# Dilated attention: class scores of exactly the blocks within reach, and class values with key tiles outside and classes inside

## The chip, the cores and the metric

The kernel runs on one NeuronCore of a Trainium2 chip. A core has TensorE for matrix products (PE in the profile, its weight loads PEld), VectorE (DVE), ScalarE (ACT), GpSimd (POOL), and the queue of SyncE (SP), which issues the DMAs of this kernel. The metric is the time of one execution in microseconds on the device; lower is better. The kernel before took 1236.35 us (median of 3 runs, 1234.39 to 1236.84).

## What is computed

One layer of a decoder for 1024 tokens of width 1024 in float32: a norm, one input projection, two mixers side by side (a gated delta rule with 4 heads of 128, and a dilated attention with 8 heads of 64), an output projection with a residual, a second norm, a gated MLP of width 2816 with a short convolution, and a last norm. The change touches the dilated attention alone. Each query at position t sees the keys of three branches, and the branches' sums are merged by their softmax denominators:

```
DIL_PATTERNS = ((128, 1), (512, 4), (2048, 16))      # (window, dilation)
...
for window, dil in DIL_PATTERNS:
    # keys t, t - dil, t - 2*dil, ... t - window, of the same head
    num, den, m = band_attention(stride(q), stride(k), stride(v), window // dil)
...
m_all = max(ms);  w_i = exp(m_i - m_all)
out = sum(w_i * num_i) / sum(w_i * den_i)
```

So a query sees all keys of the last 128 positions, and further back only keys whose distance is a multiple of 4: keys of its own class, where a token's class is its position modulo 4.

## The kernel before, in words

**Staging.** All activations lie with the channel on the partitions and the token along the free dimension. The stages follow one another on TensorE: the input projection ("dense"), the delta rule's chains, the attention, the output projection, the MLP up and down. They overlap: while the attention waits for its softmax, TensorE works on dense products that are left (the columns z of the projection, the a columns of later head pairs, and the first products of the output projection).

**The order on TensorE.** It is written out by a planner, the class Weave (line 46). Each stage is a generator that yields how long it would wait; the planner advances the ready stream with the lowest level (line 111) and books modelled costs: `product` (line 88) for TensorE, `account` (line 78) for the other engines (a fixed part and a part per element, lines 148 to 154; for ScalarE 0.12 us and 0.00085 us per element, for GpSimd 0.15 and 0.0021). A dense step is three matmuls of 512 columns (`mm3`, line 196) with a modelled 0.2135 us each. `mm` (line 188) stamps the order, so it is kept on TensorE. The slacks PSLACK and TSLACK (lines 38 and 39) let class and near values, and turns, come somewhat before the modelled time of their input. The attention has level 5, the dense products 9, the output projection 8 (lines 1491 to 1496).

**The attention** (from line 892) goes over 4 pairs of heads (pi), each with two halves of the sequence (hh = 0, 1), each half with four blocks of 128 queries (n = 4*hh + u, u = 0 to 3), taken two at a time. Inside a block the tokens are stored class by class, 32 tokens to a class. `advance` (line 1004) runs a pipeline: turn the pair before, score this pair, then the values of the pair before. The steps:

- `scores` (904): for each block, each head e of the pair against the near keys (the block and the one before it, up to 256 keys). The far keys are taken by class: 4 classes of 32 queries each against the same class of the earlier blocks, `far` columns, with weights of 64x32 at eight places of the array (line 924). `far` is 64*(n//2): 0, 0, 64, 64, 128, 128, 192, 192 for n = 0 to 7. A block with even n thereby also scores the class keys of block n - 1, which its near keys hold already; the mask puts these 32 columns to minus 1e30.
- `softmax` (929): VectorE adds the mask `mk` to the scores and finds the row's extreme in one instruction over `wd` = far + near columns, ScalarE takes the exponential with a sum, VectorE scales by the reciprocal. `mk` (line 1523) is 896 columns wide, one row of factors for even n and one for odd n.
- `turn` (946): transposes on TensorE in tiles of 128 columns into a bank; VectorE copies the near part to `pt`, ScalarE copies the far part, one instruction for all far tiles, 128 partitions, to `pb` (line 963). The tile `pb` holds for each head the far probabilities [key of class, u, key tile b, query], with one key tile for hh = 0 and two for hh = 1.
- `values` (966): the near values into the bank `po` (weights 128x64: one head's 64 channels).
- `merge_classes` (975): at the end of a group of four blocks, the class values are added to `po`: for each class c, for each part (key tile b, rows of it, first block u), for each head. For hh = 0 there is one part (64 rows, blocks 2 and 3); for hh = 1 two (tile 0: 128 rows, four blocks; tile 1: 64 rows, blocks 2 and 3).
- `give` (989): VectorE copies `po` out, SP writes it to the DRAM tensor `mixer`.

The tiles `pb` have four slots (tag "qa"), two tiles to a group, so a group's slots come free with the class values of the group before last.

Lines 139 and 141 are the planner's two calls to an engine, and 189 and 193 the two stamps of a product and a transpose; so the profile's rows are told apart by the tiles' names, not by lines. A bank of PSUM has the name `ps` in the attention's rows: `ps<-pb,vc` is a class value, `ps<-pt,vn` a near value, `ps<-kT,qT` a score, `ps<-ident,sm` a transpose, `ps<-xhi,whi`, `ps<-xlo,whi` and `ps<-xhi,wlo` the dense products.

Of the kernel before, what the change touches and what calls it, by code (L numbers as in the profile page):

```python
# [15 lines left out]
P = 128  # L16
# [5 lines left out]
NEG = -1.0e30  # L22
# [122 lines left out]
def hybrid_layer(tc, I, out):  # L145
# [22 lines left out]
    def A(name, tag, dt=F32, shape=(P, 1024)):  # L168
        if tag in TURNS:
            i = turns[tag] = turns.get(tag, -1) + 1  # L170
            tag = TURNS[tag][i % len(TURNS[tag])]
        return tile_(lp, shape, dt, name, tag, SLOTS[tag])
# [719 lines left out]
    def attention():  # L892
        for h in range(2):
            yield from wv.until(("c", h, NCH - 1))
        mk = A("mk", "go", shape=(P, 896))
        sy.dma_start(mk, I["mk"])
        for h in range(H):
            yield from wv.until(("o", h))
        for g in range(2):
            yield from wv.until(("V", g))  # L900
        yield from wv.until(("a", 0, 1))
        cur = att_load(0)

        def scores(pair):

            for it, tag in zip(pair, ("asc", "atr")):
                n = it["n"]
                it["k0"] = max(n - 1, 0) * P
                it["near"] = (n + 1) * P - it["k0"]
                it["far"] = 64 * (n // 2)  # L910
                it["wd"] = it["far"] + it["near"]
                it["ps"] = [bank(tag) for _ in range(2)]
            yield wv.need(*pair[0]["ps"], *pair[1]["ps"], pair[0]["q"], pair[0]["k"])
            for it in pair:
                n, k0, far, wd = it["n"], it["k0"], it["far"], it["wd"]
                for e, er in enumerate(HALVES):
                    mm(it["ps"][e][:, far:wd], it["q"][er, n * P:(n + 1) * P], it["k"][er, k0:k0 + wd - far],
                       0.00085 * (wd - far))
            for it in pair:
                n, far = it["n"], it["far"]  # L920
                for c in range(4 if far else 0):
                    o = slice(32 * c, 32 * c + 32)
                    for e, er in enumerate(HALVES):
                        mm(it["ps"][e][o, :far].rearrange("p (n u) -> p n u", u=32),
                           it["q"][er, n * P + 32 * c:n * P + 32 * c + 32], by_block(it["k"])[er, :far // 32, c, :],
                           0.00022 * far, tile_position=(64 * e, 32 * c))
                softmax(it)

        def softmax(it):
            pss, wd = it.pop("ps"), it["wd"]  # L930
            sm = it["sm"] = A("sm", "dv*", shape=(P, 2, 512))
            mx = tile_(sp, [P, 4], F32, "mx", "mx", 4)
            mn, den = mx[:, :2], mx[:, 2:]
            end = 896 if it["n"] % 2 else 448
            for e in range(2):
                uv.tensor_tensor_reduce(out=sm[:, e, :wd], in0=pss[e][:, :wd], in1=mk[:, end - wd:end], scale=-0.125,
                                        scalar=-NEG, op0=OP.add, op1=OP.min, accum_out=mn[:, e:e + 1])
            for e in range(2):
                ua.activation(sm[:, e, :wd], sm[:, e, :wd], AF.Exp, bias=mn[:, e:e + 1], scale=-1.0,
                              accum_out=den[:, e:e + 1])  # L940

            uv.reciprocal(den, den)
            for e in range(2):
                uv.tensor_scalar(sm[:, e, :wd], sm[:, e, :wd], den[:, e:e + 1], None, op0=OP.mult)

        def turn(pair):
            pts = A("pt", "dv*", shape=(P, 4, 256))
            for b, (it, tag) in enumerate(zip(pair, ("asc", "atr"))):
                sm, near, far = it["sm"], it["near"], it["far"]
                nf = -(-far // P)  # L950
                it["pt"] = []
                for e in range(2):
                    pt = pts[:, 2 * b + e, :]
                    it["pt"].append(pt)
                    pp = bank(tag)
                    yield wv.need(pp, sm, slack=TSLACK[b])
                    for i in range(near // P):
                        tp(pp[:, i * P:(i + 1) * P], sm[:, e, far + i * P:far + (i + 1) * P])
                    for i in range(nf):
                        tp(pp[:, near + i * P:near + (i + 1) * P], sm[:, e, i * P:(i + 1) * P])  # L960
                    uv.tensor_copy(pt[:, :near], pp[:, :near])
                    if nf:
                        ua.activation(it["pb"][e][:, it["u"], :nf, :].rearrange("p b t -> p (b t)"),
                                      pp[:, near:near + nf * P], AF.Copy)

        def values(pair):
            yield wv.need(pair[0]["po"], *pair[0]["pt"], slack=-PSLACK)
            for it in pair:
                u = it["u"]
                for i in range(it["near"] // P):  # L970
                    for e, er in enumerate(HALVES):
                        mm(it["po"][er, u * P:(u + 1) * P], v8(it["vn"])[:, it["k0"] // P + i, er],
                           it["pt"][e][:, i * P:(i + 1) * P], 0.11, u == 0 and i == 0, False, skip_group_check=True)

        def merge_classes(g):
            vcv = g["vc"].rearrange("p (b c d) -> p b c d", b=2, c=4)
            po, hh = g["po"], g["hh"]
            yield wv.need(*g["pb"], slack=-PSLACK)


            parts = (((0, 128, 0), (1, 64, 2)) if hh else ((0, 64, 2),))
            for c in range(4):
                for b, rows, u in parts:
                    for e, er in enumerate(HALVES):
                        mm(po[er].rearrange("p (u t) -> p u t", u=4)[:, u:, 32 * c:32 * c + 32],
                           vcv[:rows, b, c, er], g["pb"][e][:rows, u:, b, 32 * c:32 * c + 32], 0.11 - 0.028 * u,
                           False, c == 3 and b == hh, skip_group_check=True)

        def give(g):
            po, hh = g["po"], g["hh"]  # L990
            oT = tile_(sp, [P, 512], F32, "oT", "t2", 2)
            ve.tensor_copy(oT.rearrange("p (n u c) -> p n c u", n=4, c=4),
                           po.rearrange("p (n c u) -> p n c u", n=4, c=4))
            if g["pi"] < 3 or hh == 0:
                sy.dma_start(mixer[4 + g["pi"]][:, half(hh)], oT)
            else:
                last["oT"] = oT
            if hh == 1:
                wv.done.add(("o", 4 + g["pi"]))


        pipe = []

        def advance(pair):
            done = pipe.pop() if pipe else None
            if done is not None:
                yield from turn(done)
            if pair is not None:
                yield from scores(pair)
                pipe.append(pair)  # L1010
            if done is not None:
                yield from values(done)
                if done[1]["u"] == 3:
                    yield from merge_classes(done[0]["g"])
                    give(done[0]["g"])

        for pi in range(4):
            q, k, vn, vc = cur
            for hh in range(2):
                if hh == 1 and pi < 3:  # L1020
                    yield from wv.until(("a", pi + 1, 1))
                    cur = att_load(pi + 1)
                po = bank("ch")
                pb = [A("pb", "qa", shape=(P, 4, 1 + hh, P)) for _ in range(2)]
                if pi == 3 and hh == 1:
                    wv.done.add("last group")
                g = dict(po=po, pb=pb, hh=hh, pi=pi, vc=vc)
                for u in (0, 2):
                    yield from advance([dict(n=4 * hh + i, u=i, q=q, k=k, vn=vn, po=po, pb=pb, g=g)
                                        for i in (u, u + 1)])  # L1030
        yield from advance(None)
        wv.done.add("attention")
# [470 lines left out]
def host_inputs(inputs):  # L1503
# [5 lines left out]
    def tile_of(c):  # L1509
# [10 lines left out]
    near = levels[np.where(d < 0, 0, (d <= 128).astype(int) + (d % 4 == 0) + (d % 16 == 0))]  # L1520
    du = u32[:, None] - np.arange(32)[None, :]
    far = {e: levels[(128 * e + 4 * du <= 512).astype(int) + (du % 4 == 0)] for e in range(2, 8)}
    mk = np.concatenate([far[e] for e in range(6, 1, -1)] + [np.full((128, 32), NEG), near]
                        + [far[e] for e in range(7, 1, -1)] + [near], axis=1)
    j = np.arange(128)
    a = {
        "xT": f["x"][0].T,
# [32 lines left out]
```

## Time and profile before

| what | value |
|---|---|
| runs | 1234.39, 1236.35, 1236.84 us |
| the profiled execution's own time | 1232.33 us |
| its span, first to last instruction | 1230.2 us |
| mean granted TensorE clock | 0.995 |
| instructions | 17841, of them 6848 matmuls |
| TensorE, VectorE, ScalarE, GpSimd busy | 1206.7, 948.1, 570.7, 47.9 us |

How to read the profile: times are microseconds from the span's start, and each row of a group gives line, engine, operation, what is written from what, the shape (partitions x elements), how often, the busy time, the mean duration in ns, and after the second bar the engine's idle time just before and what ended it. In the timeline a row is start, duration, and the instructions merged into it. Matmuls are pipelined and their ends are modelled, so the difference of two starts is the better measure of what one takes. In a row of a stretch, after its limits and length, stand the busy time and number of instructions of each engine, the granted clock, and the share and rate of the DMAs.

### The profile page before, as it was taken

What the parts mean: (1) busy time and instruction counts of PE and PEld (TensorE: products, weight loads), DVE (VectorE), ACT (ScalarE), POOL (GpSimd) and SP (SyncE); (2) the same over time, 40 slices, a digit from 0 to 9 for tenths busy, and PEclk for the clock granted to TensorE, in tenths of its full rate; (3) what the DMA queues carried; (4) which work ended last, traced back from release to release, by engine and by line L of the source; (5) the groups of instructions that cost most, each with busy time, mean ns of one, the idle gap of its engine ahead of it and who ended that gap; (6) DMA issues with size and microseconds to landing.
All of it is one profiled execution on the core that took longest, in us unless ns stands there. A gap on an engine that the chain in (4) does not pass through costs nothing.

```text
span 1230.2 us, 17841 instructions
## 1 busy us (share of the span) xinstructions
PE 1206.7 (98%) x6848; PEld 992.2 (81%) x6848; DVE 948.1 (77%) x1522; ACT 570.7 (46%) x1099; POOL 47.9 (4%) x34
## 2 busy tenths in 40 slices
PE   9999999999999998999999999999999999999996
PEld 7878887888877776788888888888888888788886
DVE  7675964566377768577888889889898889899875
ACT  7393344356343345455544445444454553344441
POOL 0211010003100000000000000000000000000000
PEclk9999999999999999999999999999999999999998
DMA  6325251345722403343232231231322397545623
GB/s 231 104 90 154 83 154 71 122 136 167 238 74 95 121 27 111 129 153 117 74 103 88 66 103 61 94 101 53 103 76 79 108 373 254 172 153 183 195 86 137
DMA packets 85798, 155.02 MB, mean 126 GB/s; under 512 B 21168, under 2 KB 36176, under 8 KB 85712
## 3 DMA queue, kind: packets, MB, share of 16 engines
q1 hardware_dynamic: 85712, 153.87, 38.7%
q8 instruction: 54, 0.88, 0.3%
q14 instruction: 32, 0.26, 0.1%
HBM read 117.91 MB, written 35.93 MB: 125 GB/s over the span
## 4 chain that ended last, share of the span: by engine, by line
PE 83%; DVE 9%; DMA 4%; issue 2%; ACT 2%; POOL 0%; SPq 0%; POOLq 0%; DVEq 0%; ACTq 0%
PE ps L189 43%; PE pa L189 18%; PE pc L189 9%; PE dw L189 9%; PE ps L193 3%; DVE pr L139 2%; DMA wd<-in_wd 2%; DMA r<-upark 1%; DVE x1h L139 1%; DVE wd L139 1%; DVE kT L139 1%; DVE sm L141 1%; ACT dec L139 1%; PE warm L189 1%; DVE r L139 0%
## 5 line engine op out<-in xcount | busy, mean ns | idle before, releaser
L189 PE MATMUL dw<-pr 128*128 128x512 f32 (+1 forms) x984 | 213.2, 377 | 2.6 <-DVE x1h L139 1.9
L189 PEld LDWEIGHTS dw<-pr 128*128 128x128 f32 x984 | 176.1, 188 | 38.7 <-DVE x1h L139 3.6
L189 PE MATMUL ps<-xhi,whi 128*128 128x512 f32 x384 | 160.1, 417 | 0.0
L189 PE MATMUL ps<-xhi,wlo 128*128 128x512 f32 x384 | 150.5, 392 | 0.0
L189 PE MATMUL ps<-xlo,whi 128*128 128x512 f32 x384 | 150.1, 391 | 0.0
L189 PE MATMUL pa<-T,pair 128*128 128x512 f32 x528 | 127.0, 389 | 0.0
L189 PEld LDWEIGHTS pa<-T,pair 128*128 128x128 f32 x528 | 99.0, 188 | 20.5
L189 PEld LDWEIGHTS ps<-xhi,wlo 128*128 128x128 f32 x384 | 72.2, 188 | 16.1 <-DVE wlo L139 0.3
L189 PEld LDWEIGHTS ps<-xhi,whi 128*128 128x128 f32 x384 | 72.4, 189 | 14.9 <-issue 2.6
L189 PEld LDWEIGHTS ps<-xlo,whi 128*128 128x128 f32 x384 | 72.6, 189 | 11.2
L139 ACT ACTIVATE u<-pa 128x512 f32<-128x512 f32 x44 | 26.3, 598 | 110.7 <-PE pa L189 110.7
L139 DVE SCALAR_TENSOR_TENSOR y<-xu,fcw,y 128x1023 f32<-128x1023 f32 (+1 forms) x44 | 56.4, 1281 | 25.7 <-ACT y L139 25.6
L139 ACT ACTIVATE whi<-wst 128x1024 fp32r<-128x1024 f32 (+2 forms) x42 | 42.9, 1022 | 69.7 <-PE ps L189 64.1
L141 ACT ACTIVATE sm<-sm,mx 128x320 f32<-128x320 f32 (+4 forms) x64 | 36.1, 565 | 63.1 <-DVE mx L141 63.1
L189 PE MATMUL pc<-B,pair 128*128 128x512 f32 x264 | 63.4, 389 | 0.0
L189 PE MATMUL pa<-B,A 128*128 128x512 f32 x264 | 63.4, 389 | 0.0
L189 PE MATMUL pc<-T,S 128*128 128x512 f32 x264 | 63.4, 389 | 0.0
L189 PE MATMUL pa<-T,S 128*128 128x512 f32 x264 | 63.4, 389 | 0.0
L139 DVE TENSOR_TENSOR wst<-wst 128x512 f32<-128x512 f32 x88 | 60.4, 687 | 0.7
L189 PE MATMUL ps<-B,pair 128*128 128x512 f32 x252 | 60.5, 389 | 0.0
L139 DVE TENSOR_TENSOR wlo<-wst,whi 128x1024 fp32r<-128x1024 f32 (+2 forms) x42 | 49.4, 1175 | 12.1 <-ACT whi L139 12.0
L189 PEld LDWEIGHTS pa<-B,A 128*128 128x128 f32 x264 | 49.6, 188 | 10.3
(237 smaller groups left out, 2347.9 us busy)
## 6 DMA issues: line engine op xcount, KB each, us to landing
wst<-in_wu SPq DMA_DIRECT2D x44, 512.0 KB, 3.8
wd<-in_wd SPq DMA_DIRECT2D x44, 512.0 KB, 3.9
upark<-y SPq DMA_DIRECT2D x22, 512.0 KB, 3.8
wst<-in_wi SPq DMA_DIRECT2D x21, 512.0 KB, 3.7
r<-upark SPq DMA_DIRECT2D x11, 512.0 KB, 8.0
r<-upark SPq DMA_DIRECT2D x22, 256.0 KB, 7.0
wa<-in_wd SPq DMA_DIRECT2D x22, 256.0 KB, 2.8
wst<-in_wv SPq DMA_DIRECT2D x8, 512.0 KB, 3.6
```

The lines of the kernel that those rows point to most:

```text
L139: return getattr(eng, op)(*a, **kw)
L141: return getattr(eng, op)(*a, **kw)
L189: tc.stamp_issue_order_token(nc.tensor.matmul(dst, lhs, rhs, start=start, stop=stop, **kw).ins, TOKEN)
L193: tc.stamp_issue_order_token(nc.tensor.transpose(dst, src, ident).ins, TOKEN)
```

## The change

Four things, which belong together:

- `far` becomes 32*max(n - 1, 0): 0, 0, 32, 64, 96, 128, 160, 192 for n = 0 to 7, so class scores are made of exactly the blocks before the near ones.
- `mk` becomes 448 columns wide; the rows of even and odd n end alike, and the masked columns are gone.
- ScalarE's copy of the far part is made tile by tile, and only as many partitions as there are keys (32, 64, 96 or 128). The places of `pb` that no copy fills now, but that the class values read, are set to zero by GpSimd when the tile is taken: 32 partitions by 128 elements, once for each `pb` tile of an hh = 0 group and twice for each of an hh = 1 group.
- `merge_classes` loops over the parts outside and over the classes inside.

```diff
-        mk = A("mk", "go", shape=(P, 896))
+        mk = A("mk", "go", shape=(P, 448))
...
-                it["far"] = 64 * (n // 2)
+                it["far"] = max(n - 1, 0) * 32
...
-            end = 896 if it["n"] % 2 else 448
             for e in range(2):
-                uv.tensor_tensor_reduce(out=sm[:, e, :wd], in0=pss[e][:, :wd], in1=mk[:, end - wd:end], scale=-0.125,
+                uv.tensor_tensor_reduce(out=sm[:, e, :wd], in0=pss[e][:, :wd], in1=mk[:, 448 - wd:], scale=-0.125,
                                         scalar=-NEG, op0=OP.add, op1=OP.min, accum_out=mn[:, e:e + 1])
...
                     uv.tensor_copy(pt[:, :near], pp[:, :near])
-                    if nf:
-                        ua.activation(it["pb"][e][:, it["u"], :nf, :].rearrange("p b t -> p (b t)"),
-                                      pp[:, near:near + nf * P], AF.Copy)
+                    for i in range(nf):
+                        rows = min(far - i * P, P)
+                        ua.activation(it["pb"][e][:rows, it["u"], i, :], pp[:rows, near + i * P:near + (i + 1) * P],
+                                      AF.Copy)
...
             parts = (((0, 128, 0), (1, 64, 2)) if hh else ((0, 64, 2),))
-            for c in range(4):
-                for b, rows, u in parts:
+            for b, rows, u in parts:
+                for c in range(4):
                     for e, er in enumerate(HALVES):
                         mm(po[er].rearrange("p (u t) -> p u t", u=4)[:, u:, 32 * c:32 * c + 32],
...
                 pb = [A("pb", "qa", shape=(P, 4, 1 + hh, P)) for _ in range(2)]
                 if pi == 3 and hh == 1:
                     wv.done.add("last group")
+                for t in pb:
+                    for rows, b in (((slice(96, 128), 0), (slice(32, 64), 1)) if hh else ((slice(32, 64), 0),)):
+                        po_.memset(t[rows, 0 if b < hh else 2, b, :], 0.0)
                 g = dict(po=po, pb=pb, hh=hh, pi=pi, vc=vc)
...
-    mk = np.concatenate([far[e] for e in range(6, 1, -1)] + [np.full((128, 32), NEG), near]
-                        + [far[e] for e in range(7, 1, -1)] + [near], axis=1)
+    mk = np.concatenate([far[e] for e in range(7, 1, -1)] + [near], axis=1)
```

## The prediction

> **What bounds the kernel now.** I read the page first: how full TensorE is, and where it is not.
>
> ```profile
> span 1230.2 us, 17841 instructions
> PE 1206.7 (98%) x6848; PEld 992.2 (81%) x6848; DVE 948.1 (77%) x1522; ACT 570.7 (46%) x1099; POOL 47.9 (4%) x34
> ...
> PE   9999999999999998999999999999999999999996
> ...
> POOL 0211010003100000000000000000000000000000
> ...
> PE 83%; DVE 9%; DMA 4%; issue 2%; ACT 2%; POOL 0%; SPq 0%; POOLq 0%; DVEq 0%; ACTq 0%
> ```
>
> PE is full in nearly all of the 40 slices, and 83% of the chain that ended last is PE's. GpSimd has no work in slices 12 to 19 (338 to 584 us). The attention's place is told by the softmax's tile, and the stretches of that stage come next.
>
> ```profile
> L141 DVE CUSTOM_DVE_ANT_0 sm<-ps,mk x64: 281/520/625, 329.3 to 480.9; 128x320 f32<-128x320 f32 x16, 128x384 f32<-128x384 f32 x16, 128x448 f32<-128x448 f32 x16, 128x128 f32<-128x128 f32 x8
> ...
> core 0: us, PE busy (x) PEld busy (x) DVE busy (x) ACT busy (x) POOL busy (x), PEclk, DMA share, GB/s
> 330.00:350.00 20.00, 17.89 (x180) 13.70 (x179) 14.53 (x47) 8.40 (x29) 0.00 (x0) 0.91 0.30 106
> ...
> 341.60:467.60 126.00, 125.94 (x1183) 97.53 (x1183) 88.55 (x251) 49.08 (x144) 0.00 (x0) 0.99 0.26 81
> 467.60:487.20 19.60, 16.29 (x162) 11.92 (x152) 17.86 (x44) 11.76 (x28) 0.00 (x0) 1.00 0.26 73
> 487.20:513.70 26.50, 25.77 (x138) 20.48 (x138) 11.59 (x17) 9.20 (x15) 0.00 (x0) 1.00 0.29 102
> ```
>
> The attention's scores run from 329 to 481 us. Three parts with different limits. Near 340 us there is a stall of about 2 us, with the clock granted at 0.91 over 20 us (20 x 0.09 = 1.8 us lost). From 341.6 to 467.6 PE has no gap: what PE does less of there moves everything behind it. From 467.6 to 487.2 VectorE is the fuller engine (17.86 of 19.60) and PE idles 3.3 us; after that PE is full again. The stage's list of waits (467 to 488 us) names VectorE and ScalarE, and no DMA:
>
> ```profile
> ACT pb L141 <- DVE pt L141: 5.1, 4, 2.0
> ACT sm L141 <- DVE mx L141: 4.9, 2, 2.8
> DVE sm L141 <- PE ps L189: 3.0, 2, 1.6
> ```
>
> **The change part by part.**
>
> *Order of the class values.* Per group of four blocks with hh = 1 there are 16 products: 8 with 128 key rows (weights 128x64) and 8 with 64 key rows (64x64). A float32 product is two records. Before, two of one kind and two of the other alternate, class by class. PE's timeline:
>
> ```profile
> 346.51 1.09 PE L189 MATMUL ps<-pt,vn 128*64 128x128 f32 x16
> 347.54 0.68 PE L189 MATMUL ps<-pb,vc 64*64 64x64 f32 x16
> 348.15 0.50 PE L189 MATMUL ps<-xhi,whi 128*128 128x512 f32 x1
> ...
> 365.74 1.09 PE L189 MATMUL ps<-pt,vn 128*64 128x128 f32 x16
> 366.67 2.54 PE L189 MATMUL ps<-pb,vc 128*64 128x128 f32 x32
> 369.14 0.50 PE L189 MATMUL ps<-xhi,whi 128*128 128x512 f32 x1
> ```
>
> Ends are modelled, so I take starts. The mixed group costs 369.14 - 366.67 = 2.47 us. Its two kinds are to be seen unmixed as well: 16 records of 64x64 with both edges take 348.15 - 347.54 = 0.61 us, and 16 records of 128x64 (the near values, same shape as the class values' first kind) take 366.67 - 365.74 = 0.93 us when the same shape follows and 347.54 - 346.51 = 1.03 us when 64x64 follows. So a change of shape costs PE about 0.1 us at the edge alone, and the old order has seven such changes inside the group where the new one has one. New group: 1.03 + 0.61 = 1.64 us as the upper bound (1.03 holds an entry from the scores' shape, which the class values, coming behind equal near values, don't have), 0.93 + 0.61 = 1.54 us as the lower. Saved 0.83 to 0.93 us; I take 0.88. Four groups (hh = 1 of four head pairs): **-3.5 us**. The hh = 0 groups have one kind and stay. Three groups lie in 341.6 to 467.6, the fourth opens the full stretch at 487.2.
>
> *Class scores.* The block with even n gets 32 keys fewer (n = 2, 4, 6). The rows of the queries' tile over exactly the class scores of pairs (2,3), (4,5) and (6,7):
>
> ```profile
> 337.02:337.41 0.39, 0.39 (x34) 1.00 1.14 415
> 345.92:346.51 0.60, 0.60 (x34) 1.00 0.00 0
> 355.60:356.41 0.81, 0.81 (x34) 1.00 0.00 0
> ```
>
> 64, 128 and 192 keys on both blocks cost 0.39, 0.60 and 0.81: 0.21 us per 64 keys on two blocks, 0.05 per 32 keys on one. The step from 64 to 32 keys is seen nowhere; between nothing and 0.05. Four head pairs: 4 x (2 x 0.05 to 3 x 0.05) = 0.4 to 0.6; I take **-0.5 us**, near the middle.
>
> *Softmax width, and the copies of the turned class scores.*
>
> ```profile
> L141 DVE CUSTOM_DVE_ANT_0 sm<-ps,mk 128x448 f32<-128x448 f32 x16 | 9.0, 621 | 9.3 <-PE ps L189 9.3
> L141 DVE CUSTOM_DVE_ANT_0 sm<-ps,mk 128x320 f32<-128x320 f32 x16 | 6.9, 487 | 8.1 <-PE ps L189 8.1
> L141 DVE TENSOR_SCALAR sm<-sm,mx 128x448 f32<-128x448 f32 x16 | 6.5, 450 | 0.3
> L141 DVE TENSOR_SCALAR sm<-sm,mx 128x320 f32<-128x320 f32 x16 | 5.5, 383 | 0.2
> L141 ACT ACTIVATE pb<-ps 128x128 f32<-128x128 f32 x32 | 8.9, 277 | 23.6 <-DVE pt L141 22.9
> L141 ACT ACTIVATE pb<-ps 128x256 f32<-128x256 f32 x16 | 5.7, 382 | 7.5 <-DVE pt L141 7.3
> ```
>
> Reducing: (621 - 487) / 128 = 1.05 ns an element, 34 ns for 32; scaling: 67 / 128, 17 ns. 24 of each: VectorE is spared 1.2 us. That counts only where it is the bound, in pairs (4,5) and (6,7) of the last head pair: 2 x (2 x 34 + 2 x 17 ns) = 0.2 us. ScalarE's exponentials shrink too, beside VectorE's reducing. Its 16 copies of 256 become 32 of 128: 2 x 277 - 382 = 172 ns more each, 2.8 us in all, on an engine that is busy 49.08 of 126.00 us in the full stretch. Cover: the dense products between a turn and the scores that need its banks. Without cover stands the last merge: its two copies end just as PE comes.
>
> ```profile
> 487.15 0.71 ACT L141 ACTIVATE pb<-ps 128x256 f32<-128x256 f32 x2 [2.00 <-DVE pt L141]
> ...
> 487.89 2.64 PE L189 MATMUL ps<-pb,vc 128*64 128x128 f32 x31
> ```
>
> They end at 487.86; four shorter ones end up to 0.34 us later, so the merge waits 0 to 0.34 us; I take 0.2. Against VectorE's 0.2 that is **0**. The transposes stay at the same number.
>
> *Zeros.* 24 memsets of 32x128 (2 per hh = 0 group, 4 per hh = 1). GpSimd's own:
>
> ```profile
> L139 POOL MEMSET x<- 128x1024 f32 x2 | 1.9, 954 | 17.7 <-DVE mt L139 16.0 <-DMA xtdram<-mt 1.7
> L139 POOL MEMSET wba<- 128x256 f32 x1 | 0.3, 311 | 0.3 <-POOLq L1552 0.3
> ```
>
> Slope (954 - 311) / 768 = 0.84 ns, so about 0.2 us each, 4.9 us on an empty engine. Each waits for the slot of the group before last; behind it in GpSimd's queue stand only further memsets and, at 592 us, a power. The class values now wait for GpSimd as well; a group lasts 19 us (class values at 347.54 and 366.67 above), and the slot comes free a group ahead of its use. Cost 0; uncovered at most the last group's four, 0.8 us.
>
> A rule speaks against this. The Trainium skill, SBUF — State Buffer, section "SBUF: two separate sides", says that GpSimd and VectorE share a port pair as an exclusive lock, so that a VectorE instruction in a two-port mode and a GpSimd one block each other for a whole instruction. VectorE beside GpSimd does show stretched instructions in this trace:
>
> ```profile
> 49.89 1.28 DVE L139 SCALAR_TENSOR_TENSOR kT<-xr,gcw,kT 128x1023 f32<-128x1023 f32 x1
> ...
> 51.68 6.76 DVE L139 SCALAR_TENSOR_TENSOR kT<-xr,gcw,kT 128x1023 f32<-128x1023 f32 x4
> ...
> 55.60 3.79 POOL L139 TENSOR_SCALAR_AFFINE_SELECT dec<-dec 128x1024 f32<-128x1024 f32 x2 [0.26 <-DMA dec<-gdram]
> ```
>
> Four instructions of 1.28 us took 6.76 while GpSimd selected: 1.6 us lost. No row here shows it against a memset. This is a rival below. The mask's table is half as wide; its one load lies ahead of the attention: 0.
>
> **Sum:** -3.5 - 0.5 + 0 = -4.0 us. The profiled execution took 1232.33 us (span 1230.2 and 2.1 around it) and would take 1228.3. It lies 4.0 us under the median of the runs shown, 1236.35 (1234.39 to 1236.84), so I apply the difference to the median: **1232.4 us**.
>
> **The rivals.**
>
> *A. PE arrives early and waits.* If the next turn's tiles were made just in time, the 0.88 us would turn into waiting. Rows of VectorE and PE around the first mixed group:
>
> ```profile
> 366.92 0.48 DVE L141 TENSOR_SCALAR sm<-sm,mx 128x128 f32<-128x128 f32 x2
> 367.90 0.61 DVE L141 TENSOR_SCALAR sm<-sm,mx 128x256 f32<-128x256 f32 x2
> ...
> 369.94 0.38 PE L193 MATMUL ps<-ident,sm 128*128 128x128 f32 x2
> ```
>
> The turn's input is ready at 367.40, used at 369.94: 2.5 us to spare, 1.6 after the change. That speaks against it. For it: the planner lets a turn come up to 1 us ahead of the modelled time. Price: three groups' saving, 2.6 us: 1235.0.
>
> *B. The filler runs out sooner (slower).* The order on PE is written by the planner from its own costs, and these change: a class score is cheaper, the extra copies cost ScalarE 0.12 us more each, so single steps of three dense products fall elsewhere. The place is the pair before the last, where dense products hide VectorE's softmax:
>
> ```profile
> 469.20:475.60 6.40, 2.74 (x7) 1.00 0.23 56
> ```
>
> Those are the products of the low part of x alone: 7 steps of three, at about 0.69 us 4.8 us. If they were used up earlier, PE would stand here, and a stall like that at 340 us brings its 1.8 us of slow clock: -4.0 + 4.8 + 1.8 = +2.6, 1239.0. It decides from six steps on (6 x 0.69 = 4.1). For it: PE already idles 3.3 us here. Against: the planner's own costs move by under 0.3 us per pair, and its price of the class values is the same in both orders. As likely as a loss of steps is a gain, up to the 3.3 us; that is the lower end of the range.
>
> *C. The lock.* The memsets block VectorE. If the last group's four and two more fell into the VectorE-bound stretch, at 0.2 us each +1.2: 1233.6. By the lock that the Trainium skill's SBUF page states, the sum would be this one. Against: their slots come free with the group before last, in the stretch that PE bounds.
>
> *D. The alternation isn't the cost.* If the gaps came from something that the new order keeps, only the scores remain: 1235.9. Against: the unmixed 64x64 group of 0.61 us.
>
> **How the numbers follow.** Forecast -4.0: 0.64, with +-1.5 for the planner's steps. A 0.12, B 0.12, C 0.05, D 0.03; the gain in the last stretch (near 1230) 0.04. A measurement of this kernel tells about 0.2% (2.5 us) from no change. Faster: forecast, C and the gain, 0.73; same: A and D, 0.15; slower: B, 0.12. The range from 1229.5 (forecast with part of the 3.3 us) to 1236.5 (A and D with the runs' scatter of 1 us) leaves out B and some of the gain.
>
> **What would show it.** The mixed groups at 1.54 to 1.64 us from their first start to the next dense product; class scores 0.05 us shorter for pairs (4,5) and (6,7); 24 memsets near 0.2 us and ScalarE with 16 more instructions; PE's idle time between 467 and 490 us still near 3.3. Wrong if the groups shorten and PE gets new gaps of the same size (A), if the filler in the last two pairs falls under 7 steps (B), or if scalings beside memsets run over 450 ns (C).

## The result, and the profile after

The changed kernel takes **1228.01 us** (median of 4 runs, 1226.48 to 1230.37); the kernel before, run beside it, 1236.18 us (4 runs, 1234.39 to 1236.84). The ratio is 0.9949, with a 95% interval of 0.9934 to 0.9964: 6.3 us less, between 4.5 and 8.2; the two medians alone are 8.2 us apart, the far end of that interval. On a second chip the same two kernels gave 0.9942 (0.9927 to 0.9957), 7.2 us less. Faster was forecast, by 4.0 us (to 1232.4, between 1229.5 and 1236.5). The median lies 1.5 us under that range; the ratio, applied to the 1236.35 us that the forecast starts from, gives 1230.0, inside it. So the sign and the main term stood and 2 to 3 us came on top. The question of the experiments is where those came from.

The first lines of the profile after, in the order in which the prediction showed those of before:

```profile
span 1228.5 us, 17935 instructions
...
PE 1204.7 (98%) x6848; PEld 993.7 (81%) x6848; DVE 948.3 (77%) x1522; ACT 571.0 (46%) x1115; POOL 51.5 (4%) x58
...
PE   9999999999999999999999999999999999999996
...
PE 81%; DVE 8%; DMA 5%; issue 2%; ACT 2%; SPq 0%; POOLq 0%; POOL 0%; DVEq 0%; ACTq 0%
```

ScalarE has its 16 instructions more, GpSimd its 24, TensorE the same 6848. The one slice that stood at 8 before (the 16th, 461 to 492 us) is now a 9. The span alone is a poor measure here: 1230.2 to 1228.5 is only 1.7 us, because this execution, the slowest of the four, has a stretch of lowered clock that the profiled execution of before has not. The stretch row after (columns as in the prediction):

```profile
580.00:600.00 20.00, 18.71 (x87) 15.47 (x86) 15.59 (x23) 10.09 (x16) 2.00 (x1) 0.91 0.28 95
```

A clock of 0.91 over 20 us costs 1.8 us, in a stage that the change does not touch; the execution on the second chip has 1.00 there and a span of 1224.6. So the attention itself is compared, from its first score to the first product of the output projection behind the last class value. The row of that stretch with TensorE's busy time alone, then clock, DMA share and rate, first of before:

```profile
328.71:490.46 161.75, 156.33 (x1472) 0.99 0.29 91
```

then of the changed kernel:

```profile
329.81:484.69 154.88, 151.85 (x1471) 0.99 0.28 91
```

The stage is 6.87 us shorter, and the row splits that: TensorE's busy time falls by 4.48, its idle time from 161.75 - 156.33 = 5.42 to 154.88 - 151.85 = 3.03, by **2.39 us**. Summing the starts of the timeline by kind of product: class values 12.53 to 8.98 (-3.55), class scores 7.17 to 6.55 (-0.62), all the rest -0.3. Where the idle time went is seen in the stretches that answer to those of the prediction:

```profile
330.00:350.00 20.00, 18.00 (x184) 13.70 (x183) 13.56 (x48) 7.47 (x26) 0.06 (x1) 0.91 0.29 104
342.00:462.00 120.00, 119.74 (x1138) 94.34 (x1138) 86.39 (x251) 48.69 (x155) 3.48 (x18) 0.99 0.26 82
462.00:484.70 22.70, 21.67 (x241) 16.45 (x239) 20.56 (x48) 13.22 (x35) 0.00 (x0) 1.00 0.28 92
484.70:510.00 25.30, 24.53 (x110) 19.95 (x108) 12.63 (x18) 10.72 (x16) 0.00 (x0) 1.00 0.34 104
```

The stall near 340 us is as it was (20.00 - 18.00 = 2.0 us, clock 0.91). The middle is full. The last stretch, in which VectorE is the fuller engine, has 22.70 - 21.67 = 1.03 us of TensorE idle where before had 3.31. The work on VectorE there is as dense as before (20.56 of 22.70, 91%; before 17.86 of 19.60, 91%), which speaks against less work as the reason. What is late in this stretch is told by the timeline of VectorE at its end; before:

```profile
484.10 0.42 DVE L141 COPY pt<-ps 128x256 f32<-128x256 f32 x1
484.43 1.22 DVE L139 TENSOR_TENSOR wlo<-wst,whi 128x1024 fp32r<-128x1024 f32 x1
485.56 1.22 DVE L139 SCALAR_TENSOR_TENSOR zz<-zz,xr 128x1024 f32<-128x1024 f32 x1
486.70 0.75 DVE L141 COPY pt<-ps 128x256 f32<-128x256 f32 x2
```

and TensorE's row that waits for it, in brackets the idle time before and what ended it:

```profile
487.17 0.87 PE L189 MATMUL ps<-pt,vn 128*64 128x128 f32 x7 [1.55 <-DVE pt L141]
```

The last near values need the two copies at 486.70, and two instructions that nobody waits for yet, the low part of a weight tile (`wlo`) and the gate (`zz`), stand ahead of them: 2.4 us. After the change only one of the two does, and then the wait is half as long. VectorE and then TensorE of the changed kernel:

```profile
480.69 1.21 DVE L139 TENSOR_TENSOR wlo<-wst,whi 128x1024 fp32r<-128x1024 f32 x1
481.82 0.75 DVE L141 COPY pt<-ps 128x256 f32<-128x256 f32 x2
482.49 1.22 DVE L139 SCALAR_TENSOR_TENSOR zz<-zz,xr 128x1024 f32<-128x1024 f32 x1
```

```profile
482.30 0.87 PE L189 MATMUL ps<-pt,vn 128*64 128x128 f32 x7 [0.81 <-DVE pt L141]
```

Neither instruction is touched by the diff. Their places depend on the planner's modelled costs, which the diff does touch. So two theories stand against each other for the extra 2.4 us: the changed **order** (the planner's bookings), or the changed **work** (narrower scores, shorter softmax, no gaps in the class values).

### The profile page after: what moved, and what is told of

Read it like the earlier page. It is cut to its first block, busy times and chain, and to the rows that moved or that the text cites. A ratio compares the mean times of both kernels' runs of the same rounds, so it can differ in the third digit from the quotient of the medians.

```text
span 1228.5 us, 17935 instructions
## 1 busy us (share of the span) xinstructions
PE 1204.7 (98%) x6848; PEld 993.7 (81%) x6848; DVE 948.3 (77%) x1522; ACT 571.0 (46%) x1115; POOL 51.5 (4%) x58
## 4 chain that ended last, share of the span: by engine, by line
PE 81%; DVE 8%; DMA 5%; issue 2%; ACT 2%; SPq 0%; POOLq 0%; POOL 0%; DVEq 0%; ACTq 0%
PE ps L189 42%; PE pa L189 19%; PE pc L189 9%; PE dw L189 8%; DMA wd<-in_wd 3%; PE ps L193 3%; DVE pr L139 2%; DMA r<-upark 2%; DVE wd L139 1%; DVE x1h L139 1%; DVE kT L139 1%; PE warm L189 1%; ACT dec L139 1%; DMA wst<-in_wu 0%; DVE sm L141 0%
## 5 line engine op out<-in xcount | busy, mean ns | idle before, releaser
L141 ACT ACTIVATE sm<-sm,mx 128x128 f32<-128x128 f32 (+7 forms) x64 | 35.5, 555 | 58.8 <-DVE mx L141 58.8
L139 ACT ACTIVATE pr<-wd 128x1024 fp32r<-128x1024 f32 x33 | 34.9, 1059 | 51.9 <-PE dw L189 23.1
```

Source lines behind the costliest of these rows:

```text
L139: return getattr(eng, op)(*a, **kw)
L141: return getattr(eng, op)(*a, **kw)
```

## The experiments

"Before" and "changed" name the kernels; each ratio is to the kernel before on the same chip in the same hour. Time in us, the difference being the ratio less 1, times the median of before there (1233 to 1236 us); class values, class scores and idle are TensorE's in the attention stage; "around" is a run's time less its span, the mean of all its runs.

| run | ratio (95%) | us | class values | class scores | idle | around |
|---|---|---|---|---|---|---|
| before | 1 | 0 | 12.53 | 7.17 | 5.42 | 2.2 |
| changed | 0.9949 (0.9934-0.9964) | -6.3 | 8.98 | 6.55 | 3.03 | 1.8 |
| e1, order of class values alone | 0.9967 (0.9954-0.9980) | -4.1 | 8.98 | 7.17 | 5.75 | 2.2 |
| e2, changed without that order | 0.9967 (0.9956-0.9977) | -4.1 | 12.53 | 6.55 | 3.37 | 1.8 |
| e3, old work, new plan | 0.9985 (0.9977-0.9994) | -1.9 | 12.54 | 7.17 | 3.59 | 2.2 |
| e4, new work, old plan | 0.9968 (0.9955-0.9982) | -3.9 | 8.98 | 6.61 | 5.61 | 1.8 |
| f1, changed again | 0.9942 (0.9927-0.9957) | -7.2 | | | 3.37 | 1.8 |
| f2, two classes at a time | 0.9948 (0.9932-0.9964) | -6.4 | 10.17 | | 3.35 | 1.8 |
| f3, one shape, alternating | 0.9930 (0.9915-0.9944) | -8.6 | 8.21 | | 3.50 | 1.8 |
| f4, one shape, parts outside | 0.9931 (0.9915-0.9948) | -8.5 | 8.21 | | 3.51 | 1.8 |
| g1, VectorE's order alone | 0.9972 (0.9961-0.9983) | -3.5 | | | 4.18 | 2.2 |
| g2, f4 and VectorE's order | 0.9913 (0.9900-0.9927) | -10.7 | | | 2.67 | 1.8 |
| g3, many zeros | 0.9942 (0.9922-0.9962) | -7.2 | | | 3.36 | 1.8 |
| h1, wide table in DRAM | 0.9939 (0.9920-0.9959) | -7.5 | | | | 1.8 |

The run times give the sizes to 1 or 2 us only (e1 and e2 together make 8.1 us, the changed kernel 6.3 to 7.2); the sizes are read in the traces, the runs say whether they agree. Idle time too has a scatter: the changed kernel itself has 3.03 and 3.37 us, because one wait of a transpose near 342 us is 0.26 us in some executions and 0.57 in others.

### The order of the class values, alone and left out (e1, e2)

e1 is the kernel before with only the loops exchanged; e2 is the changed kernel with them put back.

```diff
-            for c in range(4):
-                for b, rows, u in parts:
+            for b, rows, u in parts:
+                for c in range(4):
```

> The kernel before with the loops of the class values exchanged (key tiles outside, classes inside) and nothing else. Theory P (two causes: the shapes' edges on TensorE, and the new places of dense steps and of VectorE's work in the last stretch): TensorE's and VectorE's orders are otherwise those of before, so the class values fall from 12.5 to 9.0 us, the idle time of TensorE in the attention stays near 5.4 us, and the time falls by 3.5 us. Rival W (the idle time fell because the engines have less to do or TensorE comes earlier): the idle time falls to about 3 us here too, and the time by up to 6.

> The changed kernel with the old order of the class values (classes outside). Theory P: class values stay at 12.5 us; far scores 0.6 us less than before; idle time of TensorE in the attention near 3.0 us as in the changed kernel; together about 3.3 us faster than before and 3.5 slower than the changed kernel. Rival W predicts the same here unless TensorE's earlier arrival is what removed the idle time; then idle stays near 5.4 and the gain is under 1 us.

The group's cost goes with the loops and with nothing else. TensorE's timeline of the first mixed group, e1:

```profile
368.00 1.65 PE L189 MATMUL ps<-pb,vc 128*64 128x128 f32 x32
369.58 0.50 PE L189 MATMUL ps<-xhi,whi 128*128 128x512 f32 x1
```

and e2:

```profile
368.53 2.54 PE L189 MATMUL ps<-pb,vc 128*64 128x128 f32 x32
371.00 0.50 PE L189 MATMUL ps<-xhi,whi 128*128 128x512 f32 x1
```

Start to next start: 1.58 us against 2.47. But the idle time goes the other way: e1, which saves 3.55 of the 4.17 us of products, keeps 5.75 us idle, and e2, which saves 0.62, has 3.37. That speaks for the order of the plan.

### Work and plan apart (e3, e4)

The planner books a cost for each instruction and picks the next stream by it. e3 issues the instructions of before and books the changed kernel's costs; e4 issues those of the changed kernel and books before's. The core of e3, with `n_` overriding the length that is booked:

```diff
-            n = float(np.prod(aps[0].shape[1:]))
+            n = kw.pop("n_", float(np.prod(aps[0].shape[1:])))
...
-                           0.00022 * far, tile_position=(64 * e, 32 * c))
+                           0.00022 * 32 * max(n - 1, 0), tile_position=(64 * e, 32 * c))
...
-                uv.tensor_scalar(sm[:, e, :wd], sm[:, e, :wd], den[:, e:e + 1], None, op0=OP.mult)
+                uv.tensor_scalar(sm[:, e, :wd], sm[:, e, :wd], den[:, e:e + 1], None, op0=OP.mult, n_=pw)
...
+                    if nf > 1:
+                        wv.account("scalar", 0.12 + 0.00085 * P, [it["pb"][e]], [pp], 0.28)
...
+                for t in pb:
+                    for _ in range(1 + hh):
+                        wv.account("gpsimd", 0.15 + 0.0021 * P, [t], [], 0.28)
```

> The kernel before with the planner booking the changed kernel's costs (widths of scores and softmax, extra copies, memsets) while every instruction stays as it was: dense steps on TensorE and the order on VectorE become those of the changed kernel, the work is that of before, class values alternate. Theory P: idle time in the attention falls from 5.4 to about 3.0 us with no work removed, about 2.4 us faster than before. Rival W: idle stays near 5.4 us and the time is that of before within 0.5 us.

> The changed kernel with the planner booking the costs of the kernel before: all the work and the new order of class values as changed, but dense steps and VectorE's order as before. Theory P: idle time stays near 5.4 us; class values 9.0 and far scores 6.5 us; about 4 to 4.5 us faster than before, as predicted. Rival W: idle falls to about 3 us, 6.5 us faster.

The stage rows, e3:

```profile
329.59:489.37 159.78, 156.19 (x1471) 0.99 0.29 89
```

and e4:

```profile
329.47:485.94 156.47, 150.86 (x1471) 1.00 0.30 92
```

e3 does the old work, all of it, and idles 3.59 us. e4 does the new work and idles 5.61. With e1 and e2 that makes a table of two by two without an exception: the old plan idles 5.4 to 5.8 us, the new plan 3.0 to 3.6, whatever the work and whatever the class values' order. The order of the instructions goes with it. On TensorE and VectorE e3 has the changed kernel's order throughout, instruction by instruction. On TensorE e4 has the order of before throughout. The stretch's extra gain is an **effect of the bookings**, not of the work; e3 has it alone, 1.9 us (0.7 to 2.8). e4 has the rest alone, 3.9 us (2.2 to 5.5), which is what the prediction's sum was about. (e4's stage is some 1.4 us shorter than its products and idle time explain: its clock is 1.00 there, where before has 0.99, and 0.01 of 156 us is 1.6.)

On VectorE e4 has the order of before but for a reciprocal at 468 us and for the last 8 us of the stage, where the copies to `pt` stand in other places between a scaling, `wlo` and `zz`. The booked costs are the old ones there too, so VectorE's order is not set by the bookings alone; it changes with the instructions themselves. This order brought nothing: the last near values of e4 wait 0.75 and then 1.03 us for their copies, 1.78 together, where before waits 1.55.

The instruction lists show how little the plan moved. TensorE's order differs from before at four places, by one dense step of three products each: one more before the scores of the first head pair's blocks 4 and 5, one fewer at two later places, one more in the last head pair. On VectorE, `zz` and pieces of the attention output's split move behind the copies to `pt`.

### VectorE's order alone (g1)

g1 is the kernel before; only `wlo` and `zz` (in the diff, `late` holds the two instructions) are kept behind the last copy to `pt`, and TensorE's order is untouched.

```diff
-                    uv.tensor_copy(pt[:, :near], pp[:, :near])
+                    inst = uv.tensor_copy(pt[:, :near], pp[:, :near])
+                    if it["g"]["pi"] == 3 and it["n"] == 7 and e == 1:
+                        for name in ("wlo", "zz"):
+                            after(late[name], inst, "the class values wait for this copy")
```

> The kernel before, with TensorE's order untouched, and two of VectorE's instructions in the last stretch (the low part of an output weight, 1.2 us, and a step of the gate z, 1.2 us) kept behind the last two copies of turned near scores. Theory V (TensorE's idle time in the last stretch is set by what stands ahead of these copies in VectorE's queue): the gap of 1.55 us ahead of the last near values falls under 0.5, the idle time of the attention from 5.4 to 4.4 or less, about 1.2 us faster than before. Rival D (what matters is the one dense step that the new plan puts into the last pair): gap and time as before.

VectorE's timeline of g1:

```profile
483.83 1.40 DVE L141 COPY pt<-ps 128x256 f32<-128x256 f32 x3
485.15 1.22 DVE L139 SCALAR_TENSOR_TENSOR zz<-zz,xr 128x1024 f32<-128x1024 f32 x1
486.28 1.22 DVE L139 TENSOR_TENSOR wlo<-wst,whi 128x1024 fp32r<-128x1024 f32 x1
```

and TensorE's at the same place:

```profile
484.70 1.13 PE L189 MATMUL ps<-pt,vn 128*64 128x128 f32 x15
```

The three copies run in a row and the near values in one piece: the gap of 1.55 us is gone. The stage row of g1:

```profile
329.58:488.24 158.66, 154.48 (x1472) 1.00 0.29 87
```

158.66 - 154.48 = 4.18 us idle, 1.24 less than before; the gap's 1.55 less 0.31 that the wait near 342 us has more here. So the order of two instructions on VectorE is worth up to the whole gap; the new plan takes 1.55 - 0.81 = 0.74 us of it. The rest of the plan's 2.4 us lies in three earlier gaps of before, two ended by ScalarE's copies to `pb` and one by VectorE's scaling:

```profile
476.53 0.70 PE L189 MATMUL ps<-kT,qT 64*128 64x256 f32 x2 [0.21 <-ACT pb L141]
478.00 1.51 PE L189 MATMUL ps<-kT,qT 64*128 64x256 f32 x34 [0.77 <-ACT pb L141]
...
483.97 1.06 PE L193 MATMUL ps<-ident,sm 128*128 128x128 f32 x8 [0.65 <-DVE sm L141]
```

0.21 + 0.77 + 0.65 = 1.63. g1 keeps all three with the same lengths; in the changed kernel the scores and transposes there run without a gap of over 0.11 us. Which of the moved steps removes them was not taken apart. For the 0.65 there are two candidates of the right size: the extra dense step, which takes 0.69 us (477.79 to 478.48) just ahead of these transposes, and VectorE's step `xr`, also 0.69 us, which stands ahead of the scaling in before and in e4 and behind it in the changed kernel and in e3. g1 measured 3.5 us (2.1 to 4.8), more than its trace gives; its runs were granted 0.9957 of the clock on average, those of before beside it 0.9947, and 0.001 of 1234 us is 1.2 us, so much of the surplus is probably scatter of the clock. That is argued, not shown.

### The zeros and the lock (g3)

From the second head pair on, each zeroing is made 16 times instead of once, 294 in all.

```diff
                         po_.memset(t[rows, 0 if b < hh else 2, b, :], 0.0)
+                        for _ in range(15 if pi else 0):
+                            nc.gpsimd.memset(t[rows, 0 if b < hh else 2, b, :], 0.0)
```

> The changed kernel with each memset of the zeros from the second head pair on made 16 times, so that GpSimd works some 3.2 us per place where it worked 0.2, some 58 us in all, beside VectorE's scalings of the softmax and in the stretch that TensorE bounds. Theory N (a memset doesn't hold VectorE): the scalings keep their 450 ns at 448 columns and the time is that of the changed kernel within 1 us. Rival L (the exclusive lock on a shared port): scalings beside memsets take up to 0.2 us more each or memsets stretch; VectorE is busy some us more, and the class values come late where the zeros do.

Rows by operation (minimum, median, maximum in ns, first and last start); VectorE's scalings in f1, the changed kernel:

```profile
L141 DVE TENSOR_SCALAR sm<-sm,mx x64: 281/390/453, 331.5 to 479.1; 128x128 f32<-128x128 f32 x8, 128x256 f32<-128x256 f32 x8, 128x288 f32<-128x288 f32 x8, 128x320 f32<-128x320 f32 x8
```

the scalings and the added zeros in g3:

```profile
L141 DVE TENSOR_SCALAR sm<-sm,mx x64: 280/416/508, 332.2 to 478.2; 128x128 f32<-128x128 f32 x8, 128x256 f32<-128x256 f32 x8, 128x288 f32<-128x288 f32 x8, 128x320 f32<-128x320 f32 x8
...
L1031 POOL MEMSET pb<- x270: 196/198/424, 349.4 to 463.7; 32x128 f32 x135
```

There is contention: scalings of up to 508 ns instead of 453, zeros of up to 424 instead of 198. VectorE's copies from PSUM, the reducing instructions and those with two SBUF inputs kept their durations. The trace shows how they meet. 28 zeros are lengthened; each started while a scaling ran, and each ends 0.14 us after that scaling's end, as if it had waited for it. Zeros that start within 0.1 us of a scaling's start keep their 0.2 us; there the scaling grows: one of 384 columns, whose mean is 416 ns in the kernel before, takes up to 508. That agrees with the Trainium skill, SBUF — State Buffer, section "SBUF: two separate sides", by which a VectorE instruction in a two-port mode and a GpSimd one hold the shared ports for a whole instruction and the other waits. In the time nothing of it shows: with 16 times the zeros the ratio is 0.9942 (0.9922 to 0.9962), and that of the changed kernel in f1 is 0.9942.

### The shapes of the class values (f1 to f4)

Why does the old order cost 0.89 us a group? One theory is the shape: each change between weights of 128x64 and of 64x64 costs. Its rival is the alternation itself: products that add to the same columns of PSUM in turn. f1 is the changed kernel once more. f2 takes two classes at a time (three changes of shape inside instead of one). f3 and f4 pad the second part to 128 rows, so that all class values have one shape; GpSimd zeroes the added rows. f3 alternates class by class as before, f4 has the parts outside.

```diff
-            for b, rows, u in parts:
-                for c in range(4):
+            for cs2 in ((0, 1), (2, 3)):
+                for b, rows, u, c in [(*x, c) for x in parts for c in cs2]:
```

```diff
-            parts = (((0, 128, 0), (1, 64, 2)) if hh else ((0, 64, 2),))
-            for b, rows, u in parts:
-                for c in range(4):
+            parts = (((0, 128, 0), (1, 128, 2)) if hh else ((0, 128, 2),))
+            for c in range(4):
+                for b, rows, u in parts:
...
+                    po_.memset(t[64:128, 2:, hh, :], 0.0)
```

The second diff is f3; f4 has the same `parts` and zeros, and leaves the loops as the change has them.

> The changed kernel itself, on the same chip as the next three, to compare with. Both theories: 1.585 us for a mixed group of class values (from its first record to the next dense product), and a ratio to before like the first one, near 0.995.

> The changed kernel with the class values in two rounds of two classes: key tile 0 then tile 1 for classes 0 and 1, then the same for 2 and 3. Three changes of shape inside the group in place of one. Theory S (each change of the array's shape costs TensorE a fixed time): from 7 changes, 2.472 us, and 1 change, 1.585, a change costs 0.148 us, so the group takes 1.88 us and the kernel 1.2 us more than the changed one. Rival H (the cost comes from adding to columns of the bank that were written just before): a product of tile 1 still comes 4 products after that of tile 0 in place of 2, so most of the cost stays away, under 1.7 us.

> The changed kernel with 128 key rows for every class value (the rows that hold no key are zeros that GpSimd writes, 8 memsets more of 64x256), in the old order, classes outside. All class values then have one shape, that of the near values before them, while the order that adds twice to the same columns is kept. Theory S: no change of shape, 8 x 0.109 + 8 x 0.058 us = 1.34, with the edge to the dense products up to 1.44 us for a mixed group, and 0.46 to 0.56 us for an hh = 0 group with no entry of 0.1 us. Rival H: near 2.47 us for the mixed group.

> The changed kernel with 128 key rows for every class value as in the kernel before this one, key tiles outside. Theory S: the same 1.34 to 1.44 us as with classes outside, since nothing but the shape counts; against the changed kernel 0.15 to 0.25 us less per mixed group and 0.15 to 0.25 less per hh = 0 group, 1.2 to 2 us in all. Rival: the 8 wider memsets or the added rows cost as much, time as the changed kernel.

The first mixed group of the changed kernel, of f2, and of f3 (with its first hh = 0 group ahead):

```profile
368.15 1.66 PE L189 MATMUL ps<-pb,vc 128*64 128x128 f32 x32
369.73 0.50 PE L189 MATMUL ps<-xhi,whi 128*128 128x512 f32 x1
```

```profile
368.92 1.95 PE L189 MATMUL ps<-pb,vc 128*64 128x128 f32 x32
370.80 0.50 PE L189 MATMUL ps<-xhi,whi 128*128 128x512 f32 x1
```

```profile
347.03 0.63 PE L189 MATMUL ps<-pb,vc 128*64 128x64 f32 x16
347.59 0.50 PE L189 MATMUL ps<-xhi,whi 128*128 128x512 f32 x1
...
366.01 1.51 PE L189 MATMUL ps<-pb,vc 128*64 128x128 f32 x32
367.45 0.50 PE L189 MATMUL ps<-xhi,whi 128*128 128x512 f32 x1
```

Seven changes of shape take 2.47 us, three 1.88, one 1.58, and none 1.44, although f3 alternates between the parts on the same columns, class by class: 0.15 us for each change ((2.47 - 1.58) / 6; (2.47 - 1.88) / 4; 1.58 - 1.44) and nothing for the alternation. (The last difference is the weakest of the three: in f3 the products that end the group have another shape too.) f4 takes the same 1.44. The added zeros were 16 of 64x256, not the 8 that the expectation of f3 gives; no time of theirs shows. The Trainium skill, TensorEngine Tiling (Array Packing), section "Tiling Modes", says that a change of the tiling mode drains TensorE, and gives no price; these rows agree and price it at 0.15 us for these two shapes. f4 beats the kernel before by 8.5 us (6.4 to 10.5). Against the changed kernel its class values take 0.77 us less in the trace; the run times of f1, f3 and f4 have intervals that overlap.

### The best of it (g2)

g2 is f4 with g1's two instructions kept behind the last copy.

> The kernel with 128 key rows for every class value, key tiles outside, and the same two instructions of VectorE kept behind the last copies. Theory V: the gap of 0.82 us ahead of the last near values goes, 0.6 to 0.8 us faster than the kernel without this, ratio to before about 0.9925. Rival: the gap goes, but the weight's low part comes late for the products that need it and the time is given back there.

It idles 2.67 us in the stage and takes 1224.28 us (4 runs, 1223.33 to 1225.09), 10.7 us (9.0 to 12.3) under the kernel before: the fastest version by its ratio, with an interval that overlaps those of f3 and f4.

### The time around the span (h1)

A run's time exceeds its span by 2.2 us in the kernel before, e1, e3 and g1 (2.11 to 2.29 in all their runs), and by 1.8 (1.74 to 1.91) in every version with the change's instructions: 0.4 us that no row of the trace holds. h1 is the changed kernel with the mask's table padded to 896 columns in DRAM, and only 448 loaded.

```diff
-        sy.dma_start(mk, I["mk"])
+        sy.dma_start(mk, I["mk"][:, 448:])
```

> The changed kernel, with the mask's table in DRAM padded to 896 columns again, of which the kernel loads the last 448; every instruction of the core stays. The question is the time around the span: in all executions so far the kernel before, and every variant that keeps its wide table, takes 2.11 to 2.29 us more than its span, the changed kernel and every variant with the narrow table 1.74 to 1.91 us. Theory T (the size of that input counts, outside the span): 2.1 to 2.3 us around the span. Rival R (something that the core does, the zeros or the copies): 1.7 to 1.9 us. The span itself stays at 1223 to 1228 us by both.

1.76 to 1.88 us around the span: the size of that input is not it. What the 0.4 us hang on (the copies, the zeros, the smaller tile in SBUF) stays open.

## Why the prediction was right in sign and short in size

- **Class values, -3.5.** Measured -3.55; the group went from 2.47 to 1.58 us, inside the 1.54 to 1.64 of the prediction. The reading of before, that a change of shape and not a product is what costs, was right, and f2, for which the same reading gives a value between, lay there. The edge of "about 0.1 us" was too low: it is 0.15. The near values show only 0.10 of it ahead of the change; that the other 0.05 lies behind the change is argued, not shown. The sum came right because it used whole groups. Rival D falls with this.
- **Class scores, -0.5.** Measured -0.62. The bound "between nothing and 0.05" for the step from 64 to 32 keys was open; the queries' rows are 0.39 to 0.34 there, so that step saves its 0.05 as well, and all three pairs gain.
- **Copies and VectorE's share, 0.** The cost was mis-sized, and the 0 is partly luck. The prediction added up single durations, 2.8 us more for ScalarE. Copies that follow each other overlap: the 64 keep ScalarE busy for 14.81 us in all where the 48 took 14.54, and the last four take 0.76 us together where two took 0.71. So the last merge lost 0.05 us at most, not 0.2, and in the changed kernel its class values follow the near values without a gap. A gain from VectorE's shorter instructions doesn't show either: e4 has them, and idles as much as before.
- **Zeros, 0.** 24 of 0.2 us, as said. Wrong in the step was what stands behind them in GpSimd's queue: not "only further memsets". The first zeros stand in the delta rule's stage, ahead of powers and products of its chains, for instance (GpSimd's timeline after):

```profile
279.51 0.20 POOL L139 MEMSET pb<- 32x128 f32 x1 [39.92 <-PE ps L189]
289.63 1.64 POOL L139 TENSOR_TENSOR ms<-ms,mhalf 128x8 f32<-128x8 f32 x1 [9.92 <-DVE ms L139]
```

  They cost nothing, since GpSimd then waited 9.9 us for VectorE anyway; behind a tile that came free late, the chains could have had to wait, which no run shows. Rival C's contention exists, takes 0.10 us from a scaling at most, and doesn't show in the time (g3).
- **A, waiting in place of work.** The middle stretch is full after the change (119.74 of 120.00 us): TensorE did not run into the turns.
- **B, the filler.** None was lost where the prediction feared it: the pair before the last keeps its 7 dense steps, and behind it stand 3 in place of 2.
- **The step that failed** is the last stretch: "PE's idle time between 467 and 490 us still near 3.3", with a gain and a loss of steps held "as likely" and put at 0 in the sum. It fell to 1.0. The prediction had the right object, the planner's own costs, but priced it only as steps of filler on TensorE, up or down. It did not ask what the last near values were waiting for. The row with 1.55 us of idle time was there in the trace of before, with two instructions of 1.22 us ahead of the copy that ended it, on an engine whose order moves with the planner's costs. So the gaps of this stretch belonged to one ordering, and a new one could shorten them; the case "gain in the last stretch", near 1230, deserved more than 0.04. Which way a new order would go could not be read there: the changed kernel's wait is 0.81 us, e4's 1.78. In that sense the 2.4 us are luck of the change, and not its merit.
- **The sum now.** -3.55 - 0.62 - 2.39 in the stage and -0.4 around the span: -7.0 us, beside -6.3 (-8.2 to -4.5) and -7.2 (-9.0 to -5.3) measured. Without the plan's 2.4 and the 0.4, the sum is -4.2; e4 measures work without plan at -3.9 (2.2 to 5.5, with its 0.4 in it).

## What to carry to other kernels

A product list in which the tile shape alternated between 128x64 and 64x64 paid about 0.15 us at each change here: group by shape, or pad the smaller part with zeros to one shape, which took 1.44 us for a group in place of 1.58. Where a planner orders the engines by modelled costs, an edit to a cost can re-order instructions far from the edit: list, in the trace of before, which gaps are owed to an instruction that nobody waits for yet, and hold that as a gain or loss of its own. To separate such an effect from the work, book the one version's costs and issue the other's instructions.

## What the runs showed of the hardware

- A change of tile shape between 128x64 and 64x64 costs TensorE 0.15 us; products that alternate onto the same PSUM columns in one shape cost nothing more (1.44 us for 32 records both ways).
- 64 more rows of zeros in a product's contraction cost TensorE nothing: f3's hh = 0 group of 16 records takes 347.59 - 347.03 = 0.56 us with 128 rows; the unpadded one, which has a change of shape at its start, takes 0.61.
- GpSimd's zeros and VectorE's scalings hold each other up: 28 zeros of g3 that started while a scaling ran end 0.14 us after it (at most 424 ns in place of 198). The scalings grow by at most 0.10 us, other VectorE instructions not.
- Copies of ScalarE that follow each other overlap: four of about 0.27 us take 0.76 us together.
- The scatter between runs of one kernel goes with the granted clock: on one chip before took 1230.4 to 1231.3 us in the three runs granted 0.997, and 1235.1 to 1236.2 in the two granted 0.994. With TensorE 98% busy, 0.003 of the clock is 3.7 us, most of what this change was to be measured by. One source shows in the profiles: over 330 to 350 us, where TensorE waits 1.7 to 1.8 us near 341 us in every version, the clock is 0.91 in nine of the fourteen profiled executions and 1.00 in e4, f3, f4, g1 and g3. Lengths of this stage can be compared only at the same clock.
